# A hybrid transformer layer on one core: the context's first FFN chunk in whole fp32, between the lead's second and third product

## Chip, core and metric

The kernel runs on one core of one Trainium2 chip. The metric is the device time of one execution in microseconds (us). The kernel before takes 2495.67 us, the median of three runs (2493.99 to 2496.42).

## What is computed

One layer for 128 context tokens and 1024 latent tokens of width 1024. Both groups use the same weights, but each has its own modulation (a shift and a scale for each channel, from a conditioning vector). The layer is an FFN, a mixer, and a second FFN, and the change touches only the two FFNs:

```python
def _modulate(x, shift, scale):
    return x * (1.0 + scale) + shift

def _swiglu(h, w1, w2):
    a, b = jnp.split(h @ w1, 2, axis=-1)
    return (jax.nn.silu(a) * b) @ w2

def _layer(x, mod, lw, rope, kv_ctx):
    ...
    f1 = _swiglu(_modulate(x, sh1, sc1), lw['ffn1_w1'], lw['ffn1_w2'])
    x = _layer_norm(ALPHA * x + 0.5 * g1 * f1, lw['ln_g'][0], lw['ln_b'][0])
    mix, k, v = _mixer(_modulate(x, sh2, sc2), lw, rope, kv_ctx)
    x = _layer_norm(ALPHA * x + g2 * mix, lw['ln_g'][1], lw['ln_b'][1])
    f2 = _swiglu(_modulate(x, sh3, sc3), lw['ffn2_w1'], lw['ffn2_w2'])
    x = _layer_norm(ALPHA * x + 0.5 * g3 * f2, lw['ln_g'][2], lw['ln_b'][2])
    return x, k, v
```

`w1` is 1024 x 5632 (2 x 2816), `w2` is 2816 x 1024, all in fp32.

## The kernel before

**Products in parts.** A product of fp32 matrices is made of three products in the type fp32r. Each operand is split (`split`, L106) into a high part, copied by ScalarE (L107), and a low part, the difference, by VectorE (L108). `mm3` (L127) then multiplies high by high (L130), high by low (L131) and low by high (L132) into one PSUM bank. `wide` (L387) makes the parts of a weight tile in operand tiles named `op`.

**Latent tokens: seven products.** The up products of the 1024 latent tokens use a Strassen-like scheme with seven products of half size. Their operands on the token side are called A11, A12, S1, S2, S3, S4 and A22. x comes transposed in pieces of 128 channels x 512 tokens: eight early pieces (n = 0) and eight late ones (n = 1). Each is modulated by ScalarE (L402) into a tile `xp`, `xm` or `pc` and split. In the second FFN x comes from DRAM row by row, so that `piece_dram` (L420) loads it into a raw tile and lets TensorE transpose it (L135) into a bank first. On the weight side sums and differences of halves of w1 are needed; VectorE makes them (L711 and L738 in the lead) in tiles `ts`.

**Raw tiles.** Weights and x pieces are loaded by SyncE's DMA queue (L111) into one pool of five tiles of 128x1024, named `raw` (L113). A load waits until the last reader of the tile's previous content is done. The queue issues its loads in one fixed order, so that a load that waits holds back all behind it.

**The lead.** The first four groups of w1's columns (p = 0 to 3) are done together in `lead` (L650), product by product over all four: A11 and A12 (the "first" and "second" product), then S1 (the "third"), S2, S4, S3, A22. After the second product `second` adds its bank to `s1` (L667) and applies Silu. In the first FFN the lead starts from nothing: the modulation of the first eight channel blocks is worked out in it. In the second FFN (`begun`) the first product was done earlier, within the mixer's end. The other eighteen groups follow in `up` (L765), one after another, with m = 4 to 21. `down` (L778) multiplies by w2.

**Context tokens.** The FFN of the 128 context tokens is a side generator, `ctx_ffn` (L509). Its steps are put between the main products by `tick` (L76). It goes over six chunks c of the columns of w1: eight units per chunk (`ctx_up`, L500), each of which loads a 128x1024 tile of w1 (`w1c`), splits it with `wide` and multiplies it by `mm3` into two banks. The context is the stationary operand, the weight the moving one. After Silu and product comes the chunk's part of the down product. In the first FFN this side begins after the lead, so that its steps lie in `up`; there `spare` gives a second tick after A12 for m < 15 and after S2. In the second FFN it is put up ahead of the lead, and `lead` ticks it 18 times after the second product (L702, all of chunk 0) and 5 times after the last product of p = 0 (L763).

**Who sets the order.** Each engine has one instruction queue. The program is written in the order of the loops above, and a scheduler then lays each engine's instructions in a row by its own estimate of when they are ready; tiles of a pool are given out by the same plan. So a change at one place can move instructions of other lines past each other.

Of the kernel before, what the change touches and what calls it, by code (L numbers as in the profile page):

```python
# [54 lines left out]
class Layer:  # L55
# [364 lines left out]
    def piece_dram(self, n, kc):  # L420
        r = self.raw(self.x2_d[1 + n][:, :, kc * P : (kc + 1) * P], 512)
        b = self.bank()
        for t in range(4):
            self.transpose(b[:, t * P : (t + 1) * P], r[:, t * P : (t + 1) * P])
        m = self.piece_place(n, kc)
        self.modulated(m, b, 2, LAT, kc)
        return m
# [6 lines left out]
    def open_early(self, right):  # L434

        right.close()
        tile_pool = lambda t: self.tc.tile_pool(name=f"up2_{t}", bufs=1, side="right", reuse_waits="tile")
        for t in ("ax", "xm"):
            self.pools[t] = right.enter_context(tile_pool(t))
        self.begin_operands()  # L440

        def gen():
            for kc in range(KC):
                self.first_operand(self.piece_dram, kc)
                yield
            yield from self.ctx_x_dram()

        self.add_side(gen())
# [26 lines left out]

    def ctx_operands(self):
        place = self.xm if "xm" in self.pools else self.pc
        self.xc = [(place(F32R), place(F32R)) for _ in range(2)]

    def ctx_x(self, x, i, kcs):  # L480
        for kc in kcs:
            m = self.pc()[:, :P]
            self.modulated(m, x[kc], i, CTX, kc)
            ks = slice(kc % 4 * P, (kc % 4 + 1) * P)
            self.split(self.xc[kc // 4][0][:, ks], self.xc[kc // 4][1][:, ks], m)

    def ctx_x_dram(self):
        self.ctx_operands()
        for h in range(2):
            m = self.raw(self.x2_d[0][:, h * 512 : (h + 1) * 512], 512)  # L490
            b = self.bank()
            js = [slice(j * P, (j + 1) * P) for j in range(4)]
            for j in js:
                self.transpose(b[:, j], m[:, j])
            for k, j in enumerate(js):
                self.modulated(m[:, j], b[:, j], 2, CTX, 4 * h + k)
            self.split(self.xc[h][0], self.xc[h][1], m)
            yield

    def ctx_up(self, b, w, kc, n):  # L500
        hi, lo = self.wide(self.raw(w, 2 * n), 2 * n)
        ks = slice(kc % 4 * P, (kc % 4 + 1) * P)
        xh, xl = self.xc[kc // 4]
# [5 lines left out]
    def ctx_ffn(self, i, x, w1c, w1t, w2):  # L509
        nc = self.nc  # L510
        if x:
            self.ctx_operands()
            x()
        yield
        acc = None
        for c in range(6):
            n = 256 if c == 5 else 512
            banks = [self.bank(), self.bank()]
            for kc in range(KC):
                yield from self.ctx_up(banks, w1t[kc] if c == 5 else w1c[c, kc], kc, n)  # L520
            h = self.tmp() if c == 0 and "xm" in self.pools else self.pc()
            nc.scalar.activation(h[:, :n], banks[0][:, :n], AF.Silu)
# [57 lines left out]
    def up_pair(self, m, w1, h_d):  # L580
# [16 lines left out]
        Z = self.bank()  # L597
        self.up_prod(Z, "A12", (hi[:, 512:], lo[:, 512:]), True, 1 + self.spare * (m < 15))
        add(s1, Z, s1)
# [10 lines left out]
        t34 = self.wide(ra)  # L610
        self.up_prod(Y, "S2", [halves(w)[1] for w in t12], False, 1 + self.spare)
        u2 = self.tmp()
# [37 lines left out]
    def lead(self, w1, h_d, piece, make, Y=None):  # L650
# [79 lines left out]
        else:  # L730
            for p in R:
                first_sum(p)
                X.append(self.bank())
                prod(X[p], "S1", self.wide(T[p], 512), True)
                self.next_operand(p, *S[p])
# [14 lines left out]
        for p in R:  # L750
# [10 lines left out]
            self.keep_h(p, 1, s5[p], h_d)  # L761
            if begun and p == 0:
                self.tick(5)  # L763
# [222 lines left out]
    def ffn(self, i, head, res_of, dst, order, half, beside=None, begun=None):  # L986
# [3 lines left out]
        with ExitStack() as st:  # L990
# [12 lines left out]
            context = self.ctx_ffn(i // 2, ctx_x, a["w1c_" + s], a["w1t_" + s], a["w2_" + s])  # L1003
            if begun:
                self.add_side(context)
            self.lead(a["w1_" + s], h_d, piece, make, Y)
            self.mods = mods
            if not begun:
                self.add_side(context)
            self.up(a["w1_" + s], h_d)  # L1010
# [11 lines left out]
    def head_input(self):  # L1022
        nc, a = self.nc, self.a

        def ctx_x():
            for q in range(4):
                x = self.pc()
                nc.sync.dma_start(x[:, :256], a["x_c"][q])
                self.ctx_x({q: x[:, :P], q + 4: x[:, P:256]}, 0, (q, q + 4))

        def mods():
            for part in range(2, 5):
                yield from self.mod_part(part)
# [12 lines left out]

        return self.piece_input, make, ctx_x, mods()

    def head_dram(self):
        return self.piece_dram, lambda kc: None, None, self.mod_part(8)  # L1050

# [535 lines left out]
def _layout(inputs):  # L1587
# [32 lines left out]
    for i, w in enumerate(WINDOWS):  # L1620
# [5 lines left out]
        "x_l": con(x[P:].T.reshape(KC, P, 2, 512).transpose(2, 0, 1, 3)[::-1]),  # L1626
        "x_c": con(x[:P].T.reshape(2, 4, P, P).transpose(1, 2, 0, 3)).reshape(4, P, 256),
        "w_mod": con(wm_t[16:]),
# [55 lines left out]
```

## Time and profile before

| | |
|---|---|
| median of three runs | 2495.67 us (2493.99 to 2496.42) |
| profiled execution, its own time | 2495.49 us |
| span of the profiled execution | 2493.7 us |
| mean granted clock of TensorE | 0.995 |
| TensorE (PE) busy | 2452.3 us, 98% |
| VectorE (DVE) busy | 1830.6 us, 73% |
| ScalarE (ACT) busy | 1214.5 us, 49% |
| GpSimd (POOL) busy | 463.4 us, 19% |
| loads of context chunks `raw<-w1c` | 80 of 512 KB, 4.0 us from issue to landing |

A time stamp is in us from the start of the span. PE is TensorE's matmul, PEld its weight load, SPq a DMA issue of SyncE. `w<-b,op` reads: the tile `w` (a PSUM bank) is written from `b` and `op`, with buffer numbers left out. The brackets at the end of a timeline row hold the idle time of the engine before it and what ended it.

### The profile page before, as it was taken

The numbers are of one execution on the slowest core, as the hardware profiler recorded it, in microseconds if no ns is written. First come the engines' busy times: TensorE is split into PE (matmuls) and PEld (weight loads), VectorE is DVE, ScalarE is ACT, GpSimd is POOL, SyncE is SP. The second block draws the span as 40 slices with busy tenths as digits, with TensorE's granted clock in tenths as the row PEclk, the third lists the DMA queues.
The fourth block names the chain that finished last, engine by engine and source line by source line (L and its number), as shares of the span: only waits on it lengthen the run. The fifth ranks groups of instructions, "written<-read, shape, count | busy, mean of one in ns | idle before, by whom it ended". The sixth has DMA issues, their size and how long they took to land.

```text
span 2493.7 us, 34226 instructions
## 1 busy us (share of the span) xinstructions
PE 2452.3 (98%) x12297; PEld 2115.0 (85%) x12297; DVE 1830.6 (73%) x2817; ACT 1214.5 (49%) x2094; POOL 463.4 (19%) x691
## 2 busy tenths in 40 slices
PE   8999999999999999999999999999899999999998
PEld 4788888888889989889999999998688888887887
DVE  6877778877678556566888886876877666676877
ACT  5544444444445343434778773435744344444442
POOL 0000011110022212232567640110000001111002
PEclk9999999999999999999999999999999999999999
DMA  7455566778686555534100035665754445558773
GB/s 292 144 167 188 182 224 230 244 259 326 213 276 218 184 180 189 188 136 163 42 1 2 1 110 187 237 215 185 223 173 164 150 173 195 205 197 320 269 267 121
DMA packets 167554, 463.75 MB, mean 186 GB/s; under 512 B 18900, under 2 KB 37636, under 8 KB 167384
## 3 DMA queue, kind: packets, MB, share of 16 engines
q1 hardware_dynamic: 140952, 373.79, 44.7%
q0 software_dynamic: 23696, 86.32, 9.3%
q8 instruction: 97, 1.59, 0.3%
q10 hardware_dynamic: 2736, 1.44, 0.2%
q14 instruction: 73, 0.60, 0.1%
HBM read 390.42 MB, written 71.07 MB: 185 GB/s over the span
## 4 chain that ended last, share of the span: by engine, by line
PE 84%; DVE 6%; issue 4%; DMA 3%; ACT 2%; POOL 1%; SPq 0%; DVEq 0%; POOLq 0%; ACTq 0%
PE w L130 24%; PE w L131 24%; PE w L132 24%; PE w L1060 8%; PE w L135 3%; DVE op L108 1%; DVE x L108 1%; DMA raw<-w 1%; DVE mx L1389 1%; PE w L224 0%; DMA yc<-fc 0%; ACT pr L1397 0%; DMA raw<-w1c 0%; DVE so L108 0%; DMA raw<-x 0%
## 5 line engine op out<-in xcount | busy, mean ns | idle before, releaser
L107 ACT ACTIVATE op<-raw 128x1024 fp32r<-128x1024 f32 (+1 forms) x505 | 483.9, 969 | 517.4 <-PE w L131 263.4
L108 DVE TENSOR_TENSOR op<-raw,op 128x1024 fp32r<-128x1024 f32 (+1 forms) x505 | 558.9, 1116 | 233.1 <-ACT op L107 201.1
L130 PE MATMUL w<-b,op 128*128 128x512 f32 x880 | 343.9, 393 | 7.1 <-ACT b L107 2.9
L131 PE MATMUL w<-b,op 128*128 128x512 f32 x880 | 344.6, 392 | 0.0
L132 PE MATMUL w<-b,op 128*128 128x512 f32 x880 | 339.7, 391 | 0.3 <-DVE op L108 0.3
L130 PE MATMUL w<-x,op 128*128 128x384 f32 x768 | 260.0, 339 | 0.0
L131 PE MATMUL w<-x,op 128*128 128x384 f32 x768 | 258.8, 337 | 0.0
L132 PE MATMUL w<-x,op 128*128 128x384 f32 x768 | 257.7, 337 | 0.0
L131 PE MATMUL w<-op,so 128*128 128x512 f32 (+1 forms) x627 | 242.4, 387 | 2.0 <-DVE op L108 2.0
L132 PE MATMUL w<-op,so 128*128 128x512 f32 (+1 forms) x627 | 241.9, 387 | 0.0
L130 PE MATMUL w<-op,so 128*128 128x512 f32 (+1 forms) x627 | 232.7, 386 | 1.0 <-ACT op L107 0.9
L130 PEld LDWEIGHTS w<-b,op 128*128 128x128 f32 x880 | 165.6, 188 | 42.9 <-ACT b L107 3.4
L562 POOL DMA_DIRECT2D h<-tmp x80 | 43.4, 543 | 851.6 <-DVE tmp L626 426.1
L132 PEld LDWEIGHTS w<-b,op 128*128 128x128 f32 x880 | 165.8, 188 | 35.8 <-DVE op L108 0.8
L131 PEld LDWEIGHTS w<-b,op 128*128 128x128 f32 x880 | 165.8, 188 | 34.8 <-DVE b L108 0.7
L1402 POOL TENSOR_TENSOR pr<-pr,sm 128x384 f32<-128x384 f32 x192 | 156.1, 842 | 95.1 <-DVE sm L1400 71.8
L190 DVE SCALAR_TENSOR_TENSOR junk<-raw,sil 128x1024 bf16<-128x1024 f32 x112 | 135.9, 1224 | 26.0 <-DMA raw<-w_mod 25.6
L107 ACT ACTIVATE so<-sr 128x1024 fp32r<-128x1024 f32 (+1 forms) x84 | 82.7, 986 | 136.1 <-PE w L131 82.7
L131 PEld LDWEIGHTS w<-x,op 128*128 128x128 f32 x768 | 144.1, 188 | 0.3
L130 PEld LDWEIGHTS w<-x,op 128*128 128x128 f32 x768 | 144.1, 188 | 0.4
L132 PEld LDWEIGHTS w<-x,op 128*128 128x128 f32 x768 | 143.9, 188 | 0.0
L131 PEld LDWEIGHTS w<-op,so 128*128 128x128 f32 x627 | 118.2, 189 | 26.8 <-DVE op L108 3.2
(323 smaller groups left out, 5136.6 us busy)
## 6 DMA issues: line engine op xcount, KB each, us to landing
raw<-w SPq DMA_DIRECT2D x240, 256.0 KB, 5.3
raw<-w SPq DMA_DIRECT2D x116, 512.0 KB, 3.9
raw<-w1c SPq DMA_DIRECT2D x80, 512.0 KB, 4.0
sr<-h SPq DMA_DIRECT2D x70, 512.0 KB, 5.7
raw<-w_mod SPq DMA_DIRECT2D x56, 512.0 KB, 4.3
raw<-w_gate SPq DMA_DIRECT2D x48, 512.0 KB, 3.7
h<-tmp POOLq DMA_DIRECT2D x80, 256.0 KB, 3.6
h<-pc POOLq DMA_DIRECT2D x52, 256.0 KB, 4.6
```

Source lines behind the costliest of these rows:

```text
L107: self.nc.scalar.activation(hi, src, AF.Copy)
L108: self.nc.vector.tensor_tensor(lo, src, hi.bitcast(F32), ALU.subtract)
L130: mm(out, lhsT=lh, rhs=rh, start=start, stop=False)
L131: mm(out, lhsT=lh, rhs=rl, start=False, stop=False)
L132: mm(out, lhsT=ll, rhs=rh, start=False, stop=stop)
L135: self.nc.tensor.transpose(out, src, self.ident)
L190: nc.vector.scalar_tensor_tensor(junk, w, 1.0, self.sil[cond], ALU.mult, ALU.mult, accum_out=self.mod[:, cond, b : b + 1],)
L562: self.nc.gpsimd.dma_start(h_d[f // 2][:, 2 * kh + n, f % 2, :], h)
L1060: self.nc.tensor.matmul(acc[h][j], lhsT=lhs[:, part, js], rhs=w[wi][:, h * 512 : (h + 1) * 512], start=f, stop=l)
L1389: nc.vector.tensor_reduce(mx[:, c : c + 1], b[:, :GT], AX.X, ALU.max)
L1402: nc.gpsimd.tensor_tensor(pr[:, c, :], pr[:, c, :], sm[:, 3:4].broadcast_to([P, GT]), ALU.mult)
```

## The change

- **Whole product.** In chunk 0 of both FFNs `ctx_up` multiplies the raw weight tile and the modulated context in fp32 as they are: two matmuls per unit instead of six, and no parts. Chunks 1 to 5 stay in parts.
- **Context operand.** In the first FFN x_c is loaded into two `tmp` tiles, and GpSimd modulates it in place (`ctx_whole_input`). At c = 1 it is loaded and modulated again, on ScalarE, and split (`ctx_parts_input`). In the second FFN the modulated tiles are kept and split at c = 1 (`ctx_parts_dram`).
- **Place.** In the first FFN the side is now put up ahead of the lead as well: the parts of the four S1 weights are made together, then come 18 ticks, then the S1 products; and 5 ticks after p = 0. The second ticks in `up` go down to m < 10 after A12 and none after S2. The sums of ticks agree with the steps as before.
- **Late pieces.** In the second FFN the eight late pieces are loaded into tiles of their own in the pool `b2` (name `xr`), through GpSimd's DMA queue, no longer through the raw ring and SyncE's.

The core of the diff:

```diff
     def piece_dram(self, n, kc):
-        r = self.raw(self.x2_d[1 + n][:, :, kc * P : (kc + 1) * P], 512)
+        src = self.x2_d[1 + n][:, :, kc * P : (kc + 1) * P]
+        if n == 0:
+            r = self.raw(src, 512)
+        else:
+            r = self.pools["b2"].tile([P, 512], F32, tag="b2", name=self.name("xr"), bufs=12)
+            self.nc.gpsimd.dma_start(r.rearrange("p (a b) -> p a b", a=4), src)
...
+    def ctx_whole_input(self):
+        self.xf = [self.tmp() for _ in range(2)]
+        md = self.modulators[0]
+        for h, x in enumerate(self.xf):
+            self.nc.sync.dma_start(x, self.a["x_c"][h])
+            for k in range(4):
+                js, kc = slice(k * P, (k + 1) * P), 4 * h + k
+                self.nc.gpsimd.tensor_scalar(
+                    x[:, js], x[:, js], md[:, 1, CTX, kc : kc + 1], md[:, 0, CTX, kc : kc + 1], ALU.mult, ALU.add
+                )
...
+    def ctx_parts_dram(self):
+        self.xc = []
+        for x in self.xf:
+            hi, lo = self.xm(F32R), self.pc(F32R)
+            self.split(hi, lo, x)
+            self.xc.append((hi, lo))
...
-    def ctx_up(self, b, w, kc, n):
+    def ctx_up(self, b, w, kc, n, whole):
+        ks = slice(kc % 4 * P, (kc % 4 + 1) * P)
+        if whole:
+            r = self.raw(w, 2 * n)
+            for s in range(2):
+                self.nc.tensor.matmul(
+                    b[s][:, :n], lhsT=self.xf[kc // 4][:, ks], rhs=r[:, s * n : (s + 1) * n],
+                    start=kc == 0, stop=kc == KC - 1,
+                )
+                yield
+            return
         hi, lo = self.wide(self.raw(w, 2 * n), 2 * n)
...
-        self.up_prod(Z, "A12", (hi[:, 512:], lo[:, 512:]), True, 1 + self.spare * (m < 15))
+        self.up_prod(Z, "A12", (hi[:, 512:], lo[:, 512:]), True, 1 + self.spare * (m < 10))
...
-        self.up_prod(Y, "S2", [halves(w)[1] for w in t12], False, 1 + self.spare)
+        self.up_prod(Y, "S2", [halves(w)[1] for w in t12], False)
...
             for p in R:
                 first_sum(p)
+            W = [self.wide(T[p], 512) for p in R]
+            self.tick(18)
+            for p in R:
                 X.append(self.bank())
-                prod(X[p], "S1", self.wide(T[p], 512), True)
+                prod(X[p], "S1", W[p], True)
                 self.next_operand(p, *S[p])
...
-            if begun and p == 0:
+            if p == 0:
                 self.tick(5)
...
-            if begun:
-                self.add_side(context)
+            self.add_side(context)
             self.lead(a["w1_" + s], h_d, piece, make, Y)
             self.mods = mods
-            if not begun:
-                self.add_side(context)
```

Lines move in the changed program: L667 becomes L701, L711 becomes L745, L738 becomes L775, and the fp32 product is L528.

What stands in the rows of the engines, at three places. First TensorE's row in the lead of the first FFN, at the end of the second product (`ax` are its operands) and ahead of the first S1 product; `b` are the operands of S1, `raw` a weight tile of the context. Before:

```order
L132 MATMUL w_553<-ax_494,op_343 128x512
L131 MATMUL w_568<-ax_494,op_348 128x512
L132 MATMUL w_568<-ax_494,op_348 128x512
L130 MATMUL w_225<-b_113_606,op_684 128x512
L131 MATMUL w_225<-b_113_606,op_684 128x512
L130 MATMUL w_589<-b_96_504,op_590 128x512
L131 MATMUL w_589<-b_96_504,op_590 128x512
L132 MATMUL w_589<-b_96_504,op_590 128x512
```

After, the same stretch:

```order
L132 MATMUL w_568<-ax_494,op_348 128x512
L528 MATMUL w_625<-raw_627,tmp_613 128x512
L528 MATMUL w_625<-raw_631,tmp_613 128x512
L528 MATMUL w_625<-raw_635,tmp_613 128x512
L528 MATMUL w_625<-raw_639,tmp_613 128x512
L528 MATMUL w_625<-raw_643,tmp_614 128x512
L528 MATMUL w_626<-raw_627,tmp_613 128x512
L528 MATMUL w_626<-raw_631,tmp_613 128x512
L528 MATMUL w_626<-raw_635,tmp_613 128x512
L528 MATMUL w_626<-raw_639,tmp_613 128x512
L528 MATMUL w_626<-raw_643,tmp_614 128x512
L130 MATMUL w_662<-b_96_504,op_601 128x512
```

Ten of the sixteen fp32 products stand behind the second product and ahead of S1 (`w_662`). The first S2 rows (`b_113`) no longer stand there; the first S1 rows of p = 0 come after the ten.

Second, ScalarE's row in the lead of the second FFN, where the x pieces are modulated (`pc` are late pieces) and split (`b`), and weight sums `ts` are split (`op`). Before, from the last early piece on:

```order
L402 ACTIVATE xp_17366<-w_17361,md_85 128x512
L402 ACTIVATE pc_17377<-w_17372,md_85 128x512
L402 ACTIVATE pc_17386<-w_17381,md_85 128x512
L107 ACTIVATE b_3353_17389<-pc_17377 128x512
L402 ACTIVATE pc_17405<-w_17400,md_85 128x512
L402 ACTIVATE pc_17414<-w_17409,md_85 128x512
L107 ACTIVATE b_3360_17417<-pc_17405 128x512
L402 ACTIVATE pc_17433<-w_17428,md_85 128x512
```

After, from the same piece on:

```order
L402 ACTIVATE xp_17220<-w_17215,md_85 128x512
L107 ACTIVATE op_17417<-ts_17156 128x512
L402 ACTIVATE pc_17231<-w_17226,md_85 128x512
L402 ACTIVATE pc_17240<-w_17235,md_85 128x512
L107 ACTIVATE op_17446<-ts_17156 128x512
L107 ACTIVATE b_3311_17243<-pc_17231 128x512
L402 ACTIVATE pc_17259<-w_17254,md_85 128x512
L107 ACTIVATE op_17475<-ts_17157 128x512
L402 ACTIVATE pc_17268<-w_17263,md_85 128x512
L402 ACTIVATE pc_17287<-w_17282,md_85 128x512
L107 ACTIVATE op_17504<-ts_17157 128x512
L402 ACTIVATE pc_17296<-w_17291,md_85 128x512
```

The four parts `op_17417` to `op_17504`, those of the S2 weights, now stand in between the late pieces; before, they came after all of them.

Third, SyncE's queue in the lead of the second FFN, with the engine on which each load waits; `w1c` is a weight of the context, `w_2` one of w1, `x_0` and `x_1` early and late pieces. Before, from the last context weight of chunk 0 to the first late pieces:

```order
L111 DMA raw_17308<-w_2 128x512
L111 DMA raw_17312<-w_2 128x512 [waits DMAHW6_49,DMAHW5_49,DVE_49]
L111 DMA raw_17312<-w_2 128x512
L111 DMA raw_17316<-w_2 128x512 [waits DMAHW2_49,DMAHW7_49,DMAHW1_49,DVE_49]
L111 DMA raw_17316<-w_2 128x512 [waits DMAHW0_49]
L111 DMA raw_17332<-x_0_96 128x4x128 [waits DVE_49]
L111 DMA raw_17341<-x_0_96 128x4x128 [waits DMAHW4_49,DMAHW3_49,DVE_49]
L111 DMA raw_17350<-x_0_96 128x4x128 [waits DVE_49]
L111 DMA raw_17359<-x_0_96 128x4x128 [waits DMAHW6_49,DMAHW5_49,DVE_49]
L111 DMA raw_17370<-x_1_97 128x4x128 [waits DMASW4_49,DMASW3_49,DMAHW1_49,DMASW2_49,PE_49]
L111 DMA raw_17379<-x_1_97 128x4x128 [waits DMAHW7_49,DMAHW0_49,DVE_49]
```

After, from the early pieces to the last S2 weight:

```order
L111 DMA raw_17186<-x_0_96 128x4x128 [waits PE_49]
L111 DMA raw_17195<-x_0_96 128x4x128 [waits DMAHW4_49,DMAHW3_49,DVE_49]
L111 DMA raw_17204<-x_0_96 128x4x128 [waits DMAHW6_49,DMAHW5_49,DVE_49]
L111 DMA raw_17213<-x_0_96 128x4x128 [waits PE_49]
L111 DMA raw_17349<-x_0_96 128x4x128 [waits DMAHW1_49,PE_49]
L111 DMA raw_17358<-x_0_96 128x4x128 [waits DMAHW7_49,DMAHW0_49,DVE_49]
L111 DMA raw_17367<-x_0_96 128x4x128 [waits DMAHW2_49,PE_49]
L111 DMA raw_17376<-x_0_96 128x4x128 [waits DMAHW3_49,PE_49]
L111 DMA raw_17414<-w_2 128x512 [waits DMAHW4_49,PE_49]
L111 DMA raw_17443<-w_2 128x512 [waits DMAHW1_49,DVE_49]
L111 DMA raw_17472<-w_2 128x512 [waits DMAHW2_49,DVE_49]
L111 DMA raw_17501<-w_2 128x512 [waits DMAHW3_49,DVE_49]
```

The eight loads of late pieces have left this queue. The four S2 weights (`raw_17414` to `raw_17501`) come right behind the eight early pieces, and three of them wait for VectorE.

More of the change, by code (lines that the diff above doesn't have):

```diff
@@ L445, in gen @@
                 yield
-            yield from self.ctx_x_dram()
+            yield from self.ctx_whole_dram()
         self.add_side(gen())
@@ L473, in last_operands @@
         self.A["A22"].append(self.parted(r, "b2", 12))
[L476 to L488, printed above, removed]
-        for h in range(2):
-            m = self.raw(self.x2_d[0][:, h * 512 : (h + 1) * 512], 512)
+    def ctx_whole_input(self):
[8 more added lines that the diff above has]
+                )
@@ new lines, in ctx_parts_input, with ctx_whole_dram @@
+    def ctx_parts_input(self):
+        self.xc = [(self.pc(F32R), self.pc(F32R)) for _ in range(2)]
+        for h in range(2):
+            m = self.pc()
+            self.nc.sync.dma_start(m, self.a["x_c"][h])
+            for k in range(4):
+                js = slice(k * P, (k + 1) * P)
+                self.modulated(m[:, js], m[:, js], 0, CTX, 4 * h + k)
+            self.split(self.xc[h][0], self.xc[h][1], m)
+    def ctx_whole_dram(self):
+        self.xf = []
+        for h in range(2):
+            r = self.raw(self.x2_d[0][:, h * 512 : (h + 1) * 512], 512)
@@ L491, in ctx_x_dram @@
             b = self.bank()
+            x = self.xm()
+            self.xf.append(x)
             js = [slice(j * P, (j + 1) * P) for j in range(4)]
             for j in js:
-                self.transpose(b[:, j], m[:, j])
+                self.transpose(b[:, j], r[:, j])
             for k, j in enumerate(js):
-                self.modulated(m[:, j], b[:, j], 2, CTX, 4 * h + k)
-            self.split(self.xc[h][0], self.xc[h][1], m)
+                self.modulated(x[:, j], b[:, j], 2, CTX, 4 * h + k)
@@ L501, in ctx_up @@
         hi, lo = self.wide(self.raw(w, 2 * n), 2 * n)
-        ks = slice(kc % 4 * P, (kc % 4 + 1) * P)
         xh, xl = self.xc[kc // 4]
@@ L510, in ctx_ffn @@
         nc = self.nc
-        if x:
-            self.ctx_operands()
-            x()
+        whole, parts = x
+        if whole:
+            whole()
         yield
@@ L518, in ctx_ffn @@
             banks = [self.bank(), self.bank()]
+            if c == 1:
+                parts()
             for kc in range(KC):
-                yield from self.ctx_up(banks, w1t[kc] if c == 5 else w1c[c, kc], kc, n)
-            h = self.tmp() if c == 0 and "xm" in self.pools else self.pc()
+                yield from self.ctx_up(banks, w1t[kc] if c == 5 else w1c[c, kc], kc, n, c == 0)
+            h = self.tmp() if c == 0 else self.pc()
             nc.scalar.activation(h[:, :n], banks[0][:, :n], AF.Silu)
@@ L1023, in head_input @@
         nc, a = self.nc, self.a
[L1025 to L1029, printed above, removed]
         def mods():
@@ L1045, in make @@
                 self.spread(1, rows[2:])
-        return self.piece_input, make, ctx_x, mods()
+        return self.piece_input, make, (self.ctx_whole_input, self.ctx_parts_input), mods()
     def head_dram(self):
-        return self.piece_dram, lambda kc: None, None, self.mod_part(8)
+        return self.piece_dram, lambda kc: None, (None, self.ctx_parts_dram), self.mod_part(8)
     def x2_of(self, t):
@@ L1626, in _layout @@
         "x_l": con(x[P:].T.reshape(KC, P, 2, 512).transpose(2, 0, 1, 3)[::-1]),
-        "x_c": con(x[:P].T.reshape(2, 4, P, P).transpose(1, 2, 0, 3)).reshape(4, P, 256),
+        "x_c": con(x[:P].T.reshape(2, 4, P, P).transpose(0, 2, 1, 3)).reshape(2, P, 512),
         "w_mod": con(wm_t[16:]),
```

## The prediction

> **What bounds the kernel now.** I read the page first, for the share of each engine, then the list of waits of TensorE, then the chain of work that ended last and the timeline in the two places that the change touches: the lead of each FFN. From the page:
>
> ```profile
> span 2493.7 us, 34226 instructions
> PE 2452.3 (98%) x12297; PEld 2115.0 (85%) x12297; DVE 1830.6 (73%) x2817; ACT 1214.5 (49%) x2094; POOL 463.4 (19%) x691
> ```
>
> TensorE is busy for 98% of the span. So work that is taken from ScalarE and VectorE is worth nothing by itself, work that is added to TensorE counts in full, and a gain can only come from the holes of TensorE. The change touches two groups of them. In the lead of the first FFN (timeline of TensorE, then of VectorE: start, duration, line, tile; in brackets the idle time before and what ended it):
>
> ```profile
> 60.02 0.39 PE L132 MATMUL w<-ax,op 128*128 128x512 f32 x1
> 62.03 0.50 PE L130 MATMUL w<-b,op 128*128 128x512 f32 x1 [1.62 <-ACT op L107]
> 65.52 0.79 PE L130 MATMUL w<-b,op 128*128 128x512 f32 x1 [2.52 <-DVE tmp L667]
> 66.11 0.63 PE L131 MATMUL w<-b,op 128*128 128x512 f32 x1
> 66.54 0.63 PE L132 MATMUL w<-b,op 128*128 128x512 f32 x1
> ...
> 82.37 0.39 PE L130 MATMUL w<-b,op 128*128 128x512 f32 x1
> ...
> 92.12 0.39 PE L131 MATMUL w<-b,op 128*128 128x512 f32 x1
> ```
>
> ```profile
> 60.56 0.69 DVE L738 TENSOR_TENSOR ts<-raw,ts 128x512 f32<-128x512 f32 x1
> ...
> 64.17 0.69 DVE L738 TENSOR_TENSOR ts<-raw,ts 128x512 f32<-128x512 f32 x1
> 64.78 2.48 DVE L667 TENSOR_TENSOR tmp<-w,tmp 128x512 f32<-128x512 f32 x4
> ```
>
> Between 60.4 and 65.5 TensorE does two products only. What ends the second wait is L667, the addition that empties the PSUM bank of the second product, and it stands behind a VectorE that has no gap. Afterwards products follow each other at 0.43 us until about 70, later at (92.12 - 82.37) / 43 = 0.227 us: the clock has halved after the hole.
>
> In the lead of the second FFN, the chain that ended last, in order of time (start, us, what):
>
> ```profile
> 1760.14 0.33 SPq L111
> 1760.52 3.72 DMA raw<-w
> 1764.41 0.52 issue
> 1764.93 1.23 DVE op L108
> 1766.18 4.68 DMA raw<-x
> 1770.90 0.67 PE w L135 x4
> 1771.59 0.52 SPq L111
> 1772.21 3.50 DMA raw<-x
> ...
> 1778.73 0.73 PE w L130 x2
> ...
> 1785.54 3.19 DMA raw<-w
> 1788.76 0.69 DVE ts L738
> ```
>
> Here it is no engine at all. Loads wait for a slot in the ring of five raw tiles, and a slot comes free when the reader of its last load is done: the part of a context weight (op L108) frees the slot of the first x piece (1766.18), its transposes free the next. TensorE has its last context product at 1769.0, the first product S1 at 1778.7, and no hole after 1795.
>
> **The price of an fp32 product.** The only fp32 products with 128 rows on both sides are those of the modulation (L224), 256 columns wide; each is recorded twice:
>
> ```profile
> 29.28 3.62 PE L224 MATMUL w<-wm,silt 128*2 128x256 f32 x16
> 32.83 1.20 PE L130 MATMUL w<-ax,op 128*128 128x512 f32 x4
> 1757.57 0.40 PE L130 MATMUL w<-op,xm 128*128 128x512 f32 x1
> ...
> 1767.37 0.63 PE L130 MATMUL w<-op,xm 128*128 128x512 f32 x2
> ...
> 1769.02 0.39 PE L132 MATMUL w<-op,xm 128*128 128x512 f32 x1
> ```
>
> 16 records take 32.83 - 29.28 = 3.55 us, 0.222 each; 512 columns and two records make 4 x 0.222 = 0.89 us, a little less if a part of it is fixed per record. I take 0.88. The three products that it replaces take 3 x 0.227 = 0.68 us in the first FFN. In the second, 42 steps lie between the rows 1757.57 and 1767.37 (14 units of three), 0.233 each and 0.70 for three. 16 units: +16 x 0.20 = **+3.2 us** in the first FFN, +16 x 0.18 = **+2.9 us** in the second. Nothing hides this. What goes in exchange (eight splits of 128x1024 per FFN on ScalarE and VectorE) was hidden under TensorE and is worth nothing outside the holes.
>
> **First FFN.** In the order of the changed program ten of the sixteen fp32 products stand right behind the second product, where the hole is; but the first waits for a PSUM bank, and its releaser is again that addition on VectorE (L701 now). Ahead of the addition two subtractions of weights (the L738 rows at 60.56 and 64.17) are gone, at a step of 0.61 (64.17 to 64.78): it runs at 63.6 instead of 64.8, and TensorE starts at 64.3. It loses 60.4 to 64.3, 3.9 us; before, it lost 5.1 less two products of 0.23, 4.65. Gain **0.8 us**; the slow clock follows either way. So the fp32 products stand behind the hole and not in it. After it there is no hole to fill: the row 82.37 to 92.12 is dense.
>
> The modulation of the context moves to GpSimd. The trace has no such instruction; the nearest:
>
> ```profile
> L1310 POOL TENSOR_TENSOR pl<-pl 128x296 f32<-128x296 f32 x18 | 12.4, 712 | 3.3 <-DVE dl L108 3.2
> L1117 POOL TENSOR_SCALAR rr<-ss 128x8 f32<-128x8 f32 x9 | 2.9, 317 | 94.9 <-DVE ss L1190 94.6
> ```
>
> Eight of them take between 2.5 and 5.7 us; with x_c landed by about 55 they end by 61, ahead of the bank at 64.3, and cost nothing. GPSIMD Engine Reference (Specifications) of the Trainium skill says that this engine shares its SBUF interfaces with VectorE, with contention when a VectorE instruction has two SBUF inputs, as nearly all here have. No run here shows both in this stage; were the eight twice as long by that rule, the first product would come about 2 us later and the sum be 2 us higher. Moving the eight late x loads to GpSimd's queue concerns the second FFN alone. Sum of the first FFN: +3.2 - 0.8 = **+2.4 us**, from 0.5 (two thirds of the slow clock saved) to 4.4.
>
> **Second FFN.** What replaces the waits above? The fp32 products read the raw tile itself, so a slot comes free only after the second product of its unit on TensorE, and no longer after a part on VectorE that runs ahead. I walk the order with these rows (median us from issue to landing, first in the stretch 1766 to 1775, then 1785 to 1800; products in the stretch, from the rows of tile b; one subtraction of VectorE and the first S1 products of TensorE, from their timelines):
>
> ```profile
> raw<-x SPq DMA_DIRECT2D x9, 256.0 KB, 3.9
> ...
> raw<-w SPq DMA_DIRECT2D x10, 256.0 KB, 3.2
> ```
>
> ```profile
> 1769.20:1800.00 30.80, 16.44 (x60) 10.57 (x61) 5.33 (x8) 5.46 (x10) 1.00 0.70 203
> ```
>
> ```profile
> 1764.32 0.69 DVE L711 TENSOR_TENSOR ts<-raw 128x512 f32<-128x512 f32 x1 [1.34 <-DMA raw<-w]
> ```
>
> ```profile
> 1778.73 0.73 PE L130 MATMUL w<-b,op 128*128 128x512 f32 x2 [2.25 <-ACT b L107]
> 1779.30 1.03 PE L135 MATMUL w<-ident,raw 128*128 128x128 f32 x8
> 1780.09 0.47 PE L131 MATMUL w<-b,op 128*128 128x512 f32 x1
> ```
>
> - Start at 1757.57 as before, 0.88 each: product 8 ends at 1764.6, product 16 at 1771.7.
> - The weights of S1 (two loads a tile; 4.9 us from the first issue, 1760.14, to the end of the subtraction, row 1764.32): the first after product 8, subtracted at 1769.6. The third tile waits for that subtraction, is subtracted at 1774.6 and frees the slot of the third x piece, which lands at 1778.2 (3.5, chain row 1772.21); the fourth at 1778.6, its transposes end at 1779.0.
> - The weights of S2: the first waits for those transposes; each of the other three now waits for the subtraction of the one before. A link is 3.2 + 0.7 us. Subtracted at 1783.0, 1786.9, 1790.8, 1794.7.
> - ScalarE has their parts ahead of the x pieces in its row now: the first S1 operand comes behind the second weight, the next operand behind the fourth. So the first S1 products run at 1788.2 (1778.7 before), the next at 1796.6, and only then is TensorE dense. That the eight late pieces have landed long before, on their own queue, does not help: they stand behind these parts.
> - By 1800 TensorE has done 9 products and, from 1796.6 at the slow step of 0.43, 8 more: 17 instead of 60, 43 x 0.233 = **10.0 us** behind (the +2.9 is in it).
> - Then S3: its first operand's part on VectorE stands behind three more subtractions of weights that are loaded one after another; by the same steps it comes at about 1822, TensorE arrives at 1818. Between 0 and 4.4 us; I take **2**, since loads after 1800 are quicker:
>
> ```profile
> raw<-w SPq DMA_DIRECT2D x7, 256.0 KB, 2.7
> ```
>
> Sum of the second FFN +12 us, from 7 (links of 3.2 in all, warm clock) to 17. The clock within:
>
> ```profile
> 60.00:80.00 20.00, 15.87 (x58) 12.18 (x57) 20.00 (x35) 14.44 (x27) 0.00 (x0) 0.83 0.20 60
> 1769.00:1800.00 31.00, 23.89 (x126) 17.60 (x125) 21.55 (x35) 22.00 (x35) 0.00 (x0) 1.00 0.70 203
> ```
>
> Before, the granted clock fell in the first lead (0.83) and not in the second (1.00), whose longest wait is the 2.25 us of the row 1778.73. The holes of the changed lead are some 6 us long, like the first lead's and longer. TensorE: Matmul & The Clock Gate (Part 1) of the Trainium skill says that an idle window of about 3.4 us brings the half clock back. By that rule the slow 8 products are right; by the row of the second lead alone they would be 15, and the sum 1.6 us lower.
>
> **How the numbers follow.** The profiled execution took 2495.49 us (span 2493.7), 0.2 us from the median of 2495.67. 2495.5 + 2.4 + 12 = **2510 us**; chance 0.62, own range 2502 to 2517.
>
> Rivals:
> - *The hole is filled (faster).* If ring and loads kept up, chunk and early pieces would cover the second hole. TensorE lost there, from 1769.2 to 1795, 25.8 us less some 40 products (9.3) and 64 transposes at 0.1, since the eight of the row 1779.30 end within 0.8 us (6.4): 10.1. All of it gone: 2495.5 + 2.4 + 2.9 - 10.1 = 2490.7; with the first FFN at its lower end of 0.5, **2489**. It decides if the x pieces and the second weights land before the last fp32 product, 1771.7. For it: eight of twelve pieces get slots of their own. Against: the four SP loads of pieces wait for products 14 and 16 and for two subtractions. 0.10.
> - *Only the product's price.* The serial links are hidden as well as the old ones were. With the first S1 product at 1778.7 as before the 2.9 lies in the hole, 2495.5 + 2.4 = **2498**; with TensorE losing what it lost, **2501**. It needs the first S1 product by about 1781, so the second S2 weight by 1780, when its load would not have been issued by my walk. 0.15.
> - *Links as slow as the pieces.* If each load takes 3.9 us, the four links add 2.8 us, and S3's wait is whole: **2515**, up to 2519 with GpSimd's part. 0.13.
>
> About 0.2%, 5 us, is what a measurement here can tell from no change: faster ends at 2490.7, slower begins at 2500.7. Faster 0.08; the same 0.16 (most of the second rival, the rest of the first, the low edge of the forecast); slower 0.76. The range 2497 to 2519 leaves out the first rival and the far tails.
>
> **What would show it.** fp32 products as pairs of records at a step near 0.44; in the first lead the first of them near 64.3 behind the addition; in the second lead the first S1 product near 1788 and a second hole before 1797, ended by a part on ScalarE, with the four S2 weights landing some 4 us apart; granted clock under 1 there. I am wrong if the S2 weights land together, if S1 begins before 1781, or if the fp32 products have a step of 0.23 a record.

## The result, and the profile after

The changed kernel takes **2521.14 us** (median of 4 runs, 2520.21 to 2521.43), the kernel before 2494.83 us in the same comparison (4 runs, 2493.59 to 2496.42). The ratio is 1.0104, 95% interval 1.0087 to 1.0122: 26 us slower, where some 14.5 were forecast and some 23.5 at most. The profiled execution took 2520.21 us, its span is 2518.4 us. Of the experiments below, one run of e1 (6339 us) and one of e11 (5282 us) took more than twice as long as the others and are left out of every number. From the page:

```profile
span 2518.4 us, 34119 instructions
PE 2459.1 (98%) x12265; PEld 2112.5 (84%) x12265; DVE 1813.4 (72%) x2795; ACT 1198.2 (48%) x2072; POOL 480.7 (19%) x707
```

The shares are those of before; only the span tells of the loss. To place it, two marks that both kernels have are compared: a store of x on GpSimd ahead of the second FFN (line L350), and a store of h in its `up` (L562 before, L596 after). From GpSimd's timeline (start, duration, line), before and after:

```profile
1580.19 0.53 POOL L350 DMA_DIRECT2D x<-ry  x1 [2.19 <-DVE ry L349]
1879.31 0.54 POOL L562 DMA_DIRECT2D h<-tmp  x1 [14.13 <-DVE tmp L626]
```

```profile
1580.71 0.53 POOL L350 DMA_DIRECT2D x<-ry  x1 [2.19 <-DVE ry L349]
1903.95 0.54 POOL L596 DMA_DIRECT2D h<-tmp  x1 [14.26 <-DVE tmp L660]
```

At the first mark the changed kernel is 0.5 us late, at the second 24.6. Between the marks lie 299.1 us before and 323.2 after: **24.1 us are lost in the lead of the second FFN.** Between 1757 and 1840 TensorE is idle for 25.1 us, 7.3 before. Those 17.7 us are most of the loss; the rest is the price of the fp32 products and a slower clock, and was not divided further.

The first lead, in TensorE's timeline:

```profile
58.32 0.39 PE L132 MATMUL w<-ax,op 128*128 128x512 f32 x1
62.94 11.07 PE L528 MATMUL w<-raw,tmp 128*128 128x512 f32 x20 [4.24 <-POOL tmp L488]
73.45 0.79 PE L130 MATMUL w<-b,op 128*128 128x512 f32 x1
```

The hole is still there, 4.24 us, ahead of the fp32 products and not filled by them. The profile names L488, GpSimd's modulation of x_c, as what ended it. This profile alone can't tell that from L701, the addition on VectorE: the seventh of the eight modulations ended at 62.82, the first addition at 62.84, and the first fp32 weight load started at 62.91. The kernel of e12 below has the same first FFN, and there the two lie apart (first addition, last modulation, first weight load):

```profile
62.43 0.68 DVE L701 TENSOR_TENSOR tmp<-w,tmp 128x512 f32<-128x512 f32 x1
62.82 0.44 POOL L488 TENSOR_SCALAR tmp<-tmp,md 128x128 f32<-128x128 f32 x1
63.18 0.29 PEld L528 LDWEIGHTS w<-raw,tmp 128*128 128x128 f32 x1 [4.63 <-POOL tmp L488]
```

The seventh modulation ended where the last begins, some 0.35 us before the weight load, and the last one ended after the load had begun. The addition ended at 63.11, 0.07 us ahead of it; so it does in the changed kernel and in e1, e2 and e5. The addition ended the hole, as forecast.

The first FFN ends with `down`. Its first product there (operand `so`), before and after:

```profile
556.02 0.39 PE L130 MATMUL w<-op,so 128*128 128x512 f32 x1
```

```profile
558.67 0.62 PE L130 MATMUL w<-op,so 128*128 128x512 f32 x2
```

So in this pair of profiles the first FFN costs 2.65 us up to there (2.4 forecast). Single profiles scatter by 2 us and more at such a mark. The four with before's first FFN (before, e10, e11, e14) have this product at 553.6 to 556.4, 555.3 on average; the nine with the changed one (all others but e6) have it at 557.6 to 559.6, 558.8 on average. At the first mark above the averages are 1579.2 and 1581.9. So the first FFN costs some 2.7 us at that mark, and the 0.5 us between the two profiles shown there is scatter. With the 24.1 us it makes up the 26 us measured, within that scatter.

The second lead, in the chain that ended last:

```profile
1758.24 6.88 PE w L528 x16
1765.14 0.33 SPq L111
1765.51 10.40 DMA raw<-w
1776.01 0.70 DVE ts L745
...
1778.53 5.46 DMA raw<-x
1784.12 3.75 PE w L135 x17
1787.87 4.15 DMA raw<-w
1792.05 0.70 DVE ts L775
1792.77 2.77 DMA raw<-w
1795.57 0.70 DVE ts L775
1796.29 0.63 ACT op L107
1796.92 0.61 ACT b L107
```

The chain has the links of the forecast: the product that frees a slot, a first S1 weight, an early piece, its transposes, two S2 weights one after another, their part on ScalarE (`op`), and only then the first S1 operand (`b`). But the first link took 10.40 us, where the same load took 3.72 before. TensorE's holes there, from its timeline:

```profile
1771.29 1.98 PE L528 MATMUL w<-raw,xm 128*128 128x512 f32 x4 [1.04 <-DMA raw<-w1c]
1784.12 3.70 PE L135 MATMUL w<-ident,raw 128*128 128x128 f32 x16 [10.85 <-DMA raw<-x]
...
1797.58 1.22 PE L130 MATMUL w<-b,op 128*128 128x512 f32 x2 [8.83 <-ACT b L107]
...
1826.12 0.50 PE L130 MATMUL w<-b,op 128*128 128x512 f32 x1 [1.00 <-ACT xp L402]
...
1831.62 0.50 PE L131 MATMUL w<-b,op 128*128 128x512 f32 x1 [2.26 <-DVE b L108]
```

What was in flight beside that load is told by GpSimd's timeline and by the DMA issues between 1760 and 1785 (number, KB each, median us to landing):

```profile
1760.87 5.96 POOL L426 DMA_DIRECT2D xr<-x  x8 [3.00 <-DMA x<-ry]
```

```profile
xr<-x POOLq DMA_DIRECT2D x8, 256.0 KB, 7.8
```

The eight late pieces, 2 MB in all, were issued one behind another within 6 us, the first of them 4.3 us ahead of the first S1 weight (1765.14). Three context weights of 512 KB and the other S1 weights were on their way in that stretch too, as they are in e4 below, which holds only the late pieces back. The stretch 1761 to 1776 (DMA share and GB/s at the end of the row), in the changed kernel and then in e4:

```profile
1761.00:1776.00 15.00, 11.24 (x26) 4.48 (x24) 0.00 (x0) 0.00 (x0) 5.84 (x8) 1.00 0.96 312
1761.00:1776.00 15.00, 12.14 (x29) 5.09 (x27) 2.34 (x4) 1.75 (x3) 0.00 (x0) 1.00 0.71 237
```

Granted clock and DMA share (the third and second number from the end) of the changed kernel in the stretch whose row before read 1.00 and 0.70:

```profile
1769.00:1800.00 31.00, 10.28 (x40) 6.98 (x39) 11.14 (x17) 9.27 (x15) 0.00 (x0) 0.69 0.66 202
```

### The profile page after: what moved, and what is told of

Read it like the earlier page. It is cut to its first block, busy times and chain, and to the rows that moved or that the text cites. A ratio compares the mean times of both kernels' runs of the same rounds, so it can differ in the third digit from the quotient of the medians.

```text
span 2518.4 us, 34119 instructions
## 1 busy us (share of the span) xinstructions
PE 2459.1 (98%) x12265; PEld 2112.5 (84%) x12265; DVE 1813.4 (72%) x2795; ACT 1198.2 (48%) x2072; POOL 480.7 (19%) x707
## 4 chain that ended last, share of the span: by engine, by line
PE 87%; DVE 5%; DMA 3%; issue 1%; ACT 1%; POOL 1%; SPq 0%; DVEq 0%; POOLq 0%; ACTq 0%
PE w L130 25%; PE w L131 25%; PE w L132 25%; PE w L1088 8%; PE w L135 3%; DMA raw<-w 2%; DVE op L108 1%; PE w L528 1%; DVE x L108 1%; DVE mx L1417 1%; ACT pr L1425 0%; PE w L224 0%; POOL tmp L488 0%; DMA raw<-w_mod 0%; DVE junk L190 0%
## 5 line engine op out<-in xcount | busy, mean ns | idle before, releaser
L107 ACT ACTIVATE op<-raw 128x1024 fp32r<-128x1024 f32 (+1 forms) x489 | 466.7, 966 | 529.6 <-PE w L131 266.6
L108 DVE TENSOR_TENSOR op<-raw,op 128x1024 fp32r<-128x1024 f32 (+1 forms) x489 | 539.1, 1112 | 230.4 <-ACT op L107 192.4
L596 POOL DMA_DIRECT2D h<-tmp x80 | 43.5, 544 | 819.0 <-DVE tmp L660 459.4
```

Source lines behind the costliest of these rows:

```text
L107: self.nc.scalar.activation(hi, src, AF.Copy)
L108: self.nc.vector.tensor_tensor(lo, src, hi.bitcast(F32), ALU.subtract)
L596: self.nc.gpsimd.dma_start(h_d[f // 2][:, 2 * kh + n, f % 2, :], h)
```

## The experiments

Two causes were to be told apart in the second lead: the slots, which the fp32 products hold longer, and the late pieces in places of their own. The latter were split again: the bytes in flight at the wrong time (contention), and the changed row of SyncE's queue and ScalarE, in which the S2 weights come ahead. Beside the median, each run has the time between the two marks of the second FFN, which leaves out what varies in the first.

| kernel | median us | ratio to before (95%) | between the marks |
|---|---|---|---|
| before | | | 299.1 |
| changed | 2521.14 | 1.0104 (1.0087 to 1.0122) | 323.2 |
| e1: first FFN's change alone | 2497.73 | 1.0008 (0.9998 to 1.0017) | 300.6 |
| e6: its price alone | 2499.54 | 1.0017 (1.0007 to 1.0026) | 301.3 |
| e2: whole chunk, late pieces in the ring | 2506.48 | 1.0038 (1.0025 to 1.0052) | 307.5 |
| e3: chunk in parts, late pieces in own places | 2517.20 | 1.0082 (1.0065 to 1.0099) | 319.5 |
| e4: changed, late loads held back | 2522.42 | 1.0105 (1.0090 to 1.0120) | 322.9 |
| e5: changed, early pieces behind S1 | 2506.14 | 1.0047 (1.0030 to 1.0063) | 309.2 |
| e12: changed, two of four pairs in own places | 2508.85 | 1.0051 (1.0038 to 1.0064) | 308.0 |
| e7: e1, early pieces behind S1 | 2500.96 | 1.0026 (1.0017 to 1.0036) | 302.2 |
| e9: e7, late pieces in own places on SyncE's queue | 2503.19 | 1.0033 (1.0022 to 1.0045) | 305.6 |
| e10: before, one pair in own places | 2497.64 | 1.0011 (1.0002 to 1.0019) | 302.6 |
| e11: before, two pairs in own places | 2498.90 | 1.0013 (1.0004 to 1.0022) | 303.5 |
| e14: before, two units of chunk 0 in the hole | 2494.95 | 1.0005 (0.9996 to 1.0014) | 300.3 |

Three profiles share the second FFN of before: 299.1, 300.6 and 301.3. Differences of 2 us between the marks say nothing.

**e1, the first FFN alone.** The second FFN gets back its chunk in parts and its late pieces in the ring:

```diff
-                yield from self.ctx_up(banks, w1t[kc] if c == 5 else w1c[c, kc], kc, n, c == 0)
+                yield from self.ctx_up(banks, w1t[kc] if c == 5 else w1c[c, kc], kc, n, c == 0 and i == 0)
...
-            r = self.pools["b2"].tile([P, 512], F32, tag="b2", name=self.name("xr"), bufs=12)
-            self.nc.gpsimd.dma_start(r.rearrange("p (a b) -> p a b", a=4), src)
+            r = self.raw(src, 512)
```

> First FFN as changed, second FFN as before (parts in chunk 0, late pieces through the raw ring). By the marks on GpSimd the first FFN is worth +0.5 us: 2495.3. If its share were the 2.4 us of the prediction: 2497. If the second FFN's delay were carried over from the first: over 2500.

2497.73 us, 1.7 above the 2496.01 of the kernel before beside it; the interval does not set this apart from nothing. The first FFN's part of the 26 us is some 2 us by these medians, and up to some 4 by the upper end of the interval.

**e6, the price alone.** As e1, but the context side starts behind the first lead again:

```diff
-            W = [self.wide(T[p], 512) for p in R]
-            self.tick(18)
             for p in R:
                 X.append(self.bank())
-                prod(X[p], "S1", W[p], True)
+                prod(X[p], "S1", self.wide(T[p], 512), True)
...
-            self.add_side(context)
+            if begun:
+                self.add_side(context)
             self.lead(a["w1_" + s], h_d, piece, make, Y)
+            if not begun:
+                self.add_side(context)
```

> Second FFN as before; in the first FFN chunk 0 in whole fp32, but the context side starts behind the lead as before, so that it fills no hole. Price theory of the prediction: 16 units at 0.20 us more each, +3.2 us at the end of the first FFN, 2498 to 2499. If the place in the lead had no part in the small result of the first FFN (+0.6 to +2.4 by the marks): the same as the kernel with the first FFN's change alone.

The first product of `down` comes at 559.25, 3.23 us later than before:

```profile
559.25 0.39 PE L130 MATMUL w<-op,so 128*128 128x512 f32 x1
```

That agrees with the forecast's 3.2, as far as one profile can. In e1, with the same products in the lead, it comes at 559.41, and in the nine kernels with the changed first FFN at 557.6 to 559.6. What the place in the first lead is worth is lost in that scatter. The medians leave it open as well: e6 lies 5.2 us above the kernel before beside it (2494.37) and just above the expected 2498 to 2499, e1 lies 1.7 above its own.

**e2, the whole chunk without own places; e3, own places without the whole chunk.** The two halves of e1's edit, one at a time.

> The changed kernel, but the eight late pieces go through the raw ring and SyncE's queue as before; chunk 0 stays in whole fp32. Queue theory (the late pieces' 2 MB in flight slow the loads of the S1 weights, and without them in the ring the S2 weights come ahead in a serial row): first S1 weight lands 4 to 5 us after its issue instead of 10.4, first S1 product some 6 us later than in the kernel before, about 2502. Slot theory (the fp32 products hold the raw slots, and that alone makes everything late): first S1 weight still takes about 10 us, 2512 or more.

> The changed kernel, but chunk 0 of the second FFN in parts as before; the late pieces keep their own places and GpSimd's queue. Queue theory: the S1 weights are as slow as in the changed kernel (8 to 10 us for the first), the S2 weights land one after another, about 2510. Slot theory: the slots come free early again, 2496 to 2498.

e2 loses 6 to 8 us between the marks, e3 18 to 20, and both together, in the changed kernel, 22 to 24: the parts do not add up. Both took longer than the contention theory (the queue theory of the texts above) said: e2 2506.48 us (about 2502) with the first S1 product 10 us later than before (some 6), e3 2517.20 us (about 2510). The chains (DMA links alone), e2 and then e3:

```profile
1767.83 4.54 DMA raw<-w
...
1773.57 3.64 DMA raw<-w
...
1781.62 3.05 DMA raw<-x
```

```profile
1763.66 3.83 DMA raw<-w
...
1770.14 11.86 DMA raw<-x
```

Without late pieces beside them no load of this chain takes over 4.6 us, although the fp32 products hold the slots. With them a load is slow although no fp32 product is there. The slot theory falls for the slow load. The slots still have a share of their own, the loss of e2: its first S1 weight starts to load at 1767.83, against 1760.52 before. My place for the slow load was wrong too: with parts the S1 weight is out in time (3.83) and the early piece behind it is hit (11.86).

**e4, late loads held back.** A one-column copy that reads the fourth S1 sum stands ahead of each late load on GpSimd:

```diff
+            self.nc.gpsimd.tensor_copy(r[:, :1], self.gate[:, :1])
             self.nc.gpsimd.dma_start(r.rearrange("p (a b) -> p a b", a=4), src)
```

> The changed kernel, but each late load is issued behind a one-column copy on GpSimd that reads the fourth S1 weight sum, so that no late piece is in flight while the S1 weights load. Queue theory: the first S1 weight lands in 4 to 5 us instead of 10.4, the last sum is made by 1777 instead of 1783, and the whole is 4 to 9 us shorter than the changed kernel, 2512 to 2517 (some comes back, since the late pieces now meet the early ones). Slot theory: the first S1 weight still takes 8 us or more, 2520 or longer.

The first S1 weight takes 3.99 us instead of 10.40, as the contention theory has it, but the whole is no shorter. The first S2 weight now takes 11.52:

```profile
1766.68 3.99 DMA raw<-w
...
1773.29 5.58 DMA raw<-x
...
1782.75 11.52 DMA raw<-w
```

In e3, here and in the changed kernel the 2 MB cost some 7 us where they meet the row of waits. The expected gain of 4 to 9 us did not come: the price only moved.

**e5, early pieces behind S1.** `self.first`, which the S2 operands alone need, is made behind the first S1 products:

```diff
-            self.first = [piece(0, k) for k in R]
             X = [self.bank() for _ in range(2)]
             for k in R:
                 S.append(self.sum_operands(piece, k))
...
+            self.first = [piece(0, k) for k in R]
             for p in (2, 3):
```

> The changed kernel, but the first four early pieces (needed for the S2 operands alone) are made behind the S1 sums in the program, so that ScalarE has the late pieces ahead of the S2 weight parts. Late loads stay on GpSimd's queue. If both causes hold (load contention about 7 to 8 us, the row of S2 parts the rest): the first S1 weight still takes 8 to 10 us, the first S1 product follows it at once, at 1777 to 1780, no second hole, about 2505. If contention were the whole cause: 2515 or more. If the row were the whole: below 2500.

2506.14 us, as expected from two causes. The S1 weight is as slow as in the changed kernel, but S1 starts at 1777.66, since ScalarE has no S2 part ahead of the late pieces:

```profile
1765.66 10.50 DMA raw<-w
...
1791.54 3.25 DMA raw<-w
1794.81 0.70 DVE ts L775
1795.54 2.75 DMA raw<-w
```

The S2 weights still come one by one, later and beside other work; 14 us are back (323.2 to 309.2). The edit takes the early pieces' loads from ahead of S1 as well as the S2 parts; e5 alone does not tell these two apart. With the late pieces in flight but the row out of the way the second FFN takes 309.2 between the marks, against 307.5 in e2 without them. That contention by itself costs little then is inferred, since the early pieces have moved as well.

**e12, half the bytes.** `if n == 0 or kc % 4 > 1` keeps two late pairs in the ring.

> The changed kernel with only two of the four late pairs in own places; the other two go through the raw ring, which puts the S2 weights behind the late pieces again in SyncE's queue and on ScalarE. First S1 weight 6 to 8 us (10.4 with all four pairs, 4.5 with none). If the serial row is the larger half of the change's delay: 2505 to 2509, near the 2506.5 of the ring run and far from the 2521 of the change. If contention is the larger: 2512 to 2516, half way.

The first S1 weight takes 7.01 us, between 4.54 (e2, none) and 10.40 (changed, all). The time between the marks is next to e2's (308.0 and 307.5), and 15 us of the loss are back. With two late pairs in the ring the S2 weights stand behind them again: the first S1 product comes at 1788.53, the first S2 weight starts to load at 1796.16. The early pieces are still ahead of S1. So most of what e5 gave back is put down to the row of S2 weights and not to the early pieces. Half the bytes are gone here as well, which saves 3.4 us on the slow load (10.40 less 7.01); the two shares are not separated further:

```profile
1766.70 7.01 DMA raw<-w
```

**e10 and e11, own places in the kernel before.** One or two pairs go to `xr` tiles on GpSimd's queue, and nothing else is changed.

> The kernel before, with nothing of the change but this: the first pair of late pieces (two loads, 0.5 MB) goes into tiles of its own through GpSimd's queue. Load contention by amount: 2 MB cost the load beside them some 7 us, so 0.5 MB cost 1.5 to 2 us. The order of the queues stays as before, so no serial row of S2 weights. First S1 product 1 to 3 us earlier than 1778.7, since its operands no longer wait for ring slots; 2492 to 2496. If any own place brings the serial row: 2505 or more.

> As the run before, with two pairs (four loads, 1 MB) in places of their own. Contention by amount: the load beside them some 3 to 4 us longer, which takes back what the own places give: the same as the kernel before within 3 us, 2492 to 2498. If contention were a matter of the queue and not of the bytes, as slow as the full change's loads (10 us): 2500 or more.

Neither is faster: 2497.64 and 2498.90 us are 3 to 4 us above the kernel before beside them (2494.95), and above the expected 2492 to 2496 and 2492 to 2498. The early piece that took 4.68 us before takes 7.30 beside 0.5 MB and 7.96 beside 1 MB (e10, then e11):

```profile
1765.26 7.30 DMA raw<-x
```

```profile
1766.67 7.96 DMA raw<-x
```

The first S1 product comes at 1779.96 and 1782.42, later than the 1778.73 before and not 1 to 3 us earlier. The bytes take more than the places give. For 0.5 MB I had expected 2 us at most; it was 2.6.

**e7 and e9, other orders.** e7 is e1 with e5's edit; e9 is e7 with own places, their loads on SyncE's queue (`self.load` in place of `gpsimd.dma_start`).

> First FFN as changed; second FFN with chunk 0 in parts and the late pieces through the raw ring as before, but the first four early pieces behind the S1 sums. The late pieces then take the first free raw slots: four loads at 0.9 us fewer ahead of S1, first S1 product some 3 us earlier than in the kernel with the first FFN's change alone, about 2495 against 2498 there. If the S1 weights bind instead of the pieces: no difference.

> As the run before in this list, but the late pieces have places of their own (as in the change) and are loaded through SyncE's queue, where their loads stand between those of the S1 weights instead of all at once beside them. If own places help once the loads are in order: first S1 product by 1775, hole of TensorE down from about 10 to 5 us, 2490 to 2493. If 2 MB in the same stretch cost the same in any queue: the S1 weights are late again, 2500 or more.

Neither gains anything. e7 misses its forecast (2500.96 against 2495). e9 comes out by the second branch of its own, 2500 or more. In e7 the first S1 product does come 3.7 us earlier (1777.68 against 1781.40 in e1), but the time does not follow. TensorE's granted clock between 1769 and 1800, e1 and then e7:

```profile
1769.00:1800.00 31.00, 22.83 (x118) 16.50 (x117) 20.92 (x33) 19.00 (x30) 0.00 (x0) 1.00 0.69 201
```

```profile
1769.00:1800.00 31.00, 24.34 (x110) 18.62 (x109) 20.20 (x32) 18.15 (x28) 0.00 (x0) 0.84 0.65 190
```

31 us at 0.84 instead of 1.00 are at most 5 us of work. The early pieces' transposes, which used to lie in the hole, are gone from it. That they had kept the clock up is not shown, and other profiles speak against it: e6, e10, e11 and e14 have before's order of the early pieces and were granted 0.89, 0.83, 0.83 and 0.91 there. In e9 the first late load waits on SyncE's queue for the store of x, and three of the four S1 weights behind it wait too; the third of the four lands at 1775.25 (6.15 us), and the first S1 product comes at 1777.95, not by 1775:

```profile
1762.23 3.11 DMA x<-ry
...
1769.10 6.15 DMA raw<-w
```

**e14, other work for the hole.** In the kernel before, six of the 18 ticks (two units and the chunk's end) stand behind the early pieces.

```diff
-            self.tick(18)
+            self.tick(12)
...
             self.first = [piece(0, k) for k in R]
+            self.tick(6)
```

> The kernel before; of the second FFN's chunk 0 (in parts) the last two units are put behind the first early pieces, so that their twelve products and their two loads stand in the hole ahead of S1. The S1 weights and early pieces then load earlier. If TensorE's hole can be filled by work whose loads come later: 12 x 0.233 = 2.8 us less at best, 2492 to 2494. If the loads bind there (1 MB for the two units ahead of the late pieces costs about 3 us, as 1 MB beside them did): the same, 2495 to 2498.

The same as before. None of these orders beats the kernel before.

## Why the prediction was wrong

The sign and most of the path were right, the size was not: +14.5 forecast, +26 measured, above the range.

**Price of an fp32 product: right.** 28 records took 12.18 us in one stretch, 0.435 each and 0.87 a product (0.88 forecast). For the sixteen, the one pair of profiles of e6 and before gives 3.23 us (3.2).

```profile
1758.08 12.18 PE L528 MATMUL w<-raw,xm 128*128 128x512 f32 x28
```

**First FFN: right in the sum and in the link.** It costs 2.65 us at its end in this pair of profiles and some 2.7 to 3.5 by the averages above, against +2.4. The addition L701 ended the hole; the products behind it started 1.4 us earlier than I had them (62.94 instead of 64.3), after a hole of 4.24 us (3.9). One term was mis-sized: GpSimd's eight modulations took 12.05 us, where I had put 2.5 to 5.7. The last one the hole could have waited for ended just ahead of the addition, so this cost nothing that the profiles show:

```profile
51.21 12.05 POOL L488 TENSOR_SCALAR tmp<-tmp,md 128x128 f32<-128x128 f32 x8 [48.62 <-DMA tmp<-x_c]
```

**Second FFN: this step failed.** The walk put the S1 weights at 4.9 us from issue to sum, "row 1764.32", and held that the late pieces' early landing "does not help". It hurts: the first S1 weight took 11.6 us from issue to sum (1765.14 to 1776.70), 10.40 of them the load, and e4, without late pieces beside it, 3.99 for that load. The durations of the forecast came from rows without 2 MB of late pieces beside them. The third S1 sum was to be there at 1774.6 and came at 1781.4; the transposes were to end at 1779.0 and ended at 1787.9; the first S1 product was to run at 1788.2 and ran at 1797.6. Of those 9.4 us the sums bring 6.8. The early piece behind them (5.46 us instead of 3.5) and its sixteen transposes at the slow clock (3.75 us) bring some 2 more, and the fp32 products had begun 0.5 us late (1758.08). That is most of what is missing of the 12.1 (24.1 less 12). From the sums on the walk holds: the links of S2 were 3.9 us in the forecast and 3.5 (1795.57 less 1792.05) on the chip, and between the first S1 product and the next operand's (a product at 1805.03) lay 7.5 us (8.4 forecast), which gives 1 us back. Some 2 to 3 us of the 12.1 are left that neither this nor the wait of S3 (below) accounts for.

**S3's wait: under-sized.** I took 2; TensorE waited 1.00 and 2.26 us, 3.3 in all and within my 0 to 4.4. The granted clock was 0.83 between 1830 and 1840 (1.00 before), which no term of mine held.

**The clock.** The slow step after the holes was right: 0.69 granted in the stretch, against 1.00 before. TensorE: Matmul & The Clock Gate (Part 1) of the Trainium skill says that an idle window of about 3.4 us brings the half clock back; the holes of 10.85 and 8.83 us, with 0.69 granted, agree.

**The rivals.** The nearest, links as slow as the pieces, had 2515 from 3.9 us a load. It came nearest in number, but by the wrong links: those of S2 took 3.5 us, less than forecast, and the slow load was that of S1. The one row that could have warned me was the DMA share of 0.70 with 203 GB/s in the lead before: where loads already fill most of the engines' time, 2 MB more had to be given a price.

## What to carry to other kernels

A load with a place of its own is issued without waiting for a slot, and its bytes then compete with the loads that the next product waits for. Price it by what is in flight beside it in that stage, and ask which load of the chain it will hit. When a change takes tiles out of a ring, look at what moves up in the queue in their stead: here four S2 weights moved ahead of the operands that TensorE needed first, and the two edits that undid it gave back 14 and 15 of the 24 us (e5 and e12), though each changed something else as well.

## What the runs showed of the hardware

- Beside late pieces in flight the next load of 256 KB (or pair of 256 KB) took 7.30 us with 0.5 MB, 7.01 and 7.96 with 1 MB, and 10.40 to 11.86 with 2 MB, whether a weight or a piece of x was hit. With none in flight the loads of these chains took 3.05 to 5.58 us. Other loads, of the context weights and S1, were on their way in all of these.
- GpSimd's tensor_scalar of 128x128 took 1.91 us in the median, beside VectorE operations with two inputs in SBUF. It took 0.44 beside L701, which has one input in PSUM, and 0.45 in e6 at 92.32, where VectorE did nothing:

```profile
L488 POOL TENSOR_SCALAR tmp<-tmp,md x8: 443/1912/1912, 51.2 to 62.8; 128x128 f32<-128x128 f32 x8
```

  GPSIMD Engine Reference (Specifications) of the Trainium skill says that this engine shares its SBUF interfaces with VectorE, with contention when a VectorE instruction has two SBUF inputs; these times agree. A second one of e6, at 92.75, took 0.45 with most of it beside such an instruction, so the rule is not shown for every case.
- The granted clock fell to 0.84 in e7 with no single wait of TensorE over 2.54 us between 1769 and 1784, and stayed at 1.00 in e1 with waits up to 2.25 us. In e6 it was 0.89 with a longest wait of 2.26, so the longest single wait does not settle it.
